# A one-layer hybrid kernel: its log-decay stage written in program order, weight copies a quarter later, a convolution's taps a step later, and one load moved ahead of two others

## The chip, the cores and the metric

The kernel runs on one core of one Trainium2 chip. The time is device microseconds of a whole execution, and the figure that counts is the median of several runs. Five engines work side by side, each through its own instructions in its own fixed order: PE multiplies matrices, DVE and POOL do element-wise arithmetic, ACT evaluates functions and copies, and SP issues the DMAs. An instruction that waits holds up everything behind it on its engine.

## What is computed

The reference is one transformer layer over 1024 tokens of width 1024. A gated linear attention (GLA) over chunks and a short convolution mix the tokens; a second part with a 3x3 convolution follows. The change touches the part around the attention's decay gates, which the reference states so:

```python
def gate_logdecay(a_low, w, b):
    a = (a_low @ w + b).astype(jnp.float32)
    return (jax.nn.log_sigmoid(a) / GLA_TAU).reshape(...)

def gla_final_state(k, v, g):                  # over the 256 context tokens
    b = jnp.cumsum(g.astype(jnp.float32), axis=1)
    w = jnp.exp(b[:, -1:] - b)
    return jnp.einsum('bthk,bthv->bhkv', k * w, v)

def token_mixers(p, s_f, s_b, ...):
    k, v, g_f, g_b = gla_inputs(p, ...)
    ...
    o_sc = sb * dwconv_row(sc * sx, w_sc, b_sc, rows, width)   # three taps along a row of 64
    return jnp.concatenate([o_gla, o_sc], axis=-1)             # then @ w_out
```

All matrix products that carry precision are made from two parts of each operand, a high part and a low part, with three multiplications (high by high, low by high, high by low).

## The kernel before

PE's order is written out by hand for the whole program. The other engines are ordered by a scheduler, which works from a simulated timing, except inside the `manual_schedule` blocks, where the named engines keep the order of the code.

**The stage around the change.** After the first projections two generators run side by side. `stream()` multiplies sixteen more 128-column blocks of the input projection (C_SC, C_SX and C_SB for each of four column groups j, then C_OG). `halves` runs a block: two halves of 512 tokens, each of them 24 matmuls that stop half way for a `yield`, so a block has four quarters of 12 matmuls. `gla()` computes the decays, the chunk states and the attention. After each of its steps it yields a number of quarters, and the loop at the end runs that many quarters of `stream()` in between. So PE alternates between a few small matmuls of `gla()` and 12 long ones of `stream()`.

**The log-decay steps.** Two context chunks (`ctx_decay`) and then eight chunks of tokens, c = 0 to 7 (`decay(c)`), pass through `logdecay`: PE makes 128x512 gate values in one of two banks `ps_at`; ACT applies Abs, Exp and Ln one after the other (tile `ge`); DVE makes `gc` or `g` from them, which frees the bank for the gate matmul after next. `ctx_keys(j)` lets PE sum `gc` by a triangle `tri` into a bank `ps_ms`, ACT take the exponential into `kw`, and DVE multiply. `sums(c)`, two steps behind `decay(c)`, sums `g` in a bank `ps_ms`, and ACT copies it to `bc`. There are two such banks, so each of these waits for ACT to empty the one before the last. `ctx_state` makes the start state. For the chunk states a tile `kx` is made of `bc` (DVE difference, ACT exponential, DVE product with the keys), once for each half of the tokens and each direction; PE turns it in `kx_turn` and multiplies it in `update`. `dec` holds the decays of whole chunks.

**Weights of `stream()`.** `stream_weights` loads a block (`wr`, 512 KB) while the block ahead is being multiplied, ACT copies the high part `wh`, and POOL makes the low part `wl` in four pieces, one after each quarter. There are two of each of these tiles. In the code the copy `wh` stands where the load stands, at the start of the block ahead.

**The short convolution.** `sc_first` keeps the C_SC half, `sc_conv` multiplies it by the C_SX half and applies three taps (ACT the middle one, DVE the two others), and `sc_last` multiplies by the C_SB half and stores it.

**What is ordered by hand before.** `ORDERED = 2`: DVE alone keeps the code's order for the first two steps of each generator. From there on ACT and DVE follow the scheduler.

**The output projection.** After the attention, a `manual_schedule` block of ACT, DVE and SP prepares the first two token tiles of the product with w_out: `so` (the stored convolution half of each of the two tiles, the second one in a part of `t7`), `sog` (the gate half, which passes through Silu in `mix_gate`), and the parts of w_out (`wo_split`). PE's first 24 matmuls use `so[0]`, the next 24 use `so[1]`, and only then come the products that need the gated half.

Of the kernel before, what the change touches and what calls it, by code (L numbers as in the profile page):

```python
# [21 lines left out]
P = 128  # L22
# [13 lines left out]
GW = 64  # L36
# [83 lines left out]
def build(nc, ap, out, dbg=None):  # L120
# [3 lines left out]
    def nm(s="t"):  # L124
        return f"{s}{next(names)}"

    def act(o, i, fn=AF.Copy, **kw):
        return S.activation(o, i, fn, **kw)  # L128
# [20 lines left out]
    with tile.TileContext(nc) as tc, tc.manual_schedule(engines={mybir.EngineType.PE}):  # L149
# [25 lines left out]
        def bank(n):  # L175
            return pools[n][1].tile([P, 512], F32, tag=n, name=nm("ps"))
# [7 lines left out]
        def col(name, j=0, n=1):  # L184
            o, w = COLS[name]
            return cols[:, o + j : o + j + n]
# [372 lines left out]
        def stream_weights(src, eng):  # L559
            raw = wp.tile([P, KT, P], F32, tag="wraw", name=nm("wr"))  # L560
            SY.dma_start(raw, src)
            hi = wp.tile([P, KT, P], F32R, tag="whi", name=nm("wh"))
            lo = wp.tile([P, KT, P], F32R, tag="wlo", name=nm("wl"))
            act(hi, raw)

            def rest():
                for k in range(0, KT, 2):
                    eng.tensor_tensor(lo[:, k : k + 2], raw[:, k : k + 2], hi[:, k : k + 2].bitcast(F32), ALU.subtract)  # L568
                    yield

            return hi, lo, rest()
# [67 lines left out]
        def halves(w, nxt, dests):  # L639

            hi, lo = w[:2]
            for hf in range(2):
                bk = bank(ps_mm)
                s = slice(hf * 512, hf * 512 + 512)
                for kt in range(KT):
                    mm3(bk, (hi[:, kt, :], lo[:, kt, :]), (hxh[kt][:, s], hxl[kt][:, s]), kt == 0, kt == KT - 1)
                    if kt == KT // 2 - 1:
                        next(nxt[2], None)
                        yield
                dests(hf, bk)  # L650
                next(nxt[2], None)
                yield

        def stream():
            w = w2
            for n in range(16):
# [8 lines left out]
                    yield from halves(w, nxt, lambda hf, bk: og_out(n - 12, hf, bk))  # L665
                w = nxt

        def sc_tile(dt=F32):
            return pg_.tile([P, 512], dt, tag="sc", bufs=4, name=nm("sc"))

# [4 lines left out]
        def sc_conv(j, hf, bk, us):  # L675
            u = us[hf]
            V.tensor_tensor(u, u, bk, ALU.mult)
            y = sc_tile()
            act(y, u, AF.Identity, bias=col("bsc", j), scale=col("wsc", 3 * j + 1))
            y3, u3 = (a.rearrange("p (r c) -> p r c", c=GW) for a in (y, u))  # L680
            V.scalar_tensor_tensor(y3[:, :, 1:], u3[:, :, :-1], col("wsc", 3 * j), y3[:, :, 1:], ALU.mult, ALU.add)
            V.scalar_tensor_tensor(y3[:, :, :-1], u3[:, :, 1:], col("wsc", 3 * j + 2), y3[:, :, :-1], ALU.mult, ALU.add)
            us[hf] = y

        def sc_last(j, hf, bk, us):
            y = us[hf]
# [28 lines left out]
            split(wo_raw(0), hi, lo)  # L715
            woh[worder[0]], wol[worder[0]] = hi, lo

        ORDERED = 2
        on = [None] * NT
        pe_ = popen("pe_", "right", bufs=1)  # L720
        flat = lambda t: t.rearrange("p f t -> p (f t)")
# [1 line left out]
        def gla():  # L723
# [26 lines left out]

            kxs, kxt = {}, {}

            def kx_prep(hf, d):
                e = (P - 1) if d == 0 else 0
                for hh in range(2):
                    act(decv[d * DK : d * DK + DK, hh, :, 4 * hf : 4 * hf + 4],
                        bc[hf][d][hh * DK : hh * DK + DK].rearrange("p f (c t) -> p f c t", t=P)[:, :, :, e],
                        AF.Exp, scale=ITAU)
                kx = pe_.tile([P, 2, 512], F32, tag="e", bufs=4, name=nm("kx"))
                b3 = bc[hf][d].rearrange("p f (c t) -> p (f c) t", t=P)  # L760
                V.tensor_tensor(kx.rearrange("p f (c t) -> p (f c) t", t=P),
                                b3[:, :, e : e + 1].broadcast_to([P, 8, P]), b3, ALU.subtract)
                act(kx, kx, AF.Exp, scale=ITAU)
                V.tensor_tensor(kx, kx, kh[hf], ALU.mult)
                kxs[hf, d] = kx

            def kx_turn(c):
                pt = bank(ps_at)
# [52 lines left out]
            for c in range(NT):  # L821
                decay(c)
                if c == 2:
                    V.tensor_copy(masks, mraw)
                if 0 < c <= NCT:
                    ctx_keys(c - 1)
                if c > 1:
                    sums(c - 2)
                if c == 4:
                    su = [px.tile([P, 2, 512], F32, tag="x", name=f"su{i}") for i in range(4)]  # L830
                    ctx_state()
                if c in (5, 6):
                    kx_prep(0, c - 5)
                yield 0.8 if c > 1 else 1
            sums(NT - 2)
            yield 0.8
# [1 line left out]
            for c in range(NT):  # L838
                kx_turn(c)
                if c == 1:  # L840
                    pclose("pgt")
                    pw = popen("pw", "left", bufs=1)
                    for n in range(3):
                        wo_raw(n)
                if c > 0:
                    update(c - 1)
                if c in (1, 2):
                    kx_prep(1, c - 1)
                yield 1.2
            update(NT - 1)  # L850

# [134 lines left out]
                    yield 0.8  # L986

        ga, st = gla(), stream()
        with tc.manual_schedule(engines={mybir.EngineType.DVE}):
            for _ in range(ORDERED):  # L990
                next(st)
                next(ga)
        due = 0.0
        for steps in ga:
            due += steps
            while due >= 1:
# [41 lines left out]
        def dma(dst, src):  # L1038
            behind[0] = SY.dma_start(dst, src).ins
# [7 lines left out]
        def gate_load(c):  # L1047
            sog = p2.tile([P, H, P], F32, tag="sog", bufs=2, name=nm("sog"))
            dma(sog, og_d[c // 4][c % 4])
            return sog  # L1050
# [6 lines left out]
        def mix_first(so):  # L1057
            mh = wp.tile([P, KT, P], F32R, tag="whi", name=nm("mh"))
            ml = wp.tile([P, KT, P], F32R, tag="wlo", name=nm("ml"))
            split(so, mh[:, 4:8, :], ml[:, 4:8, :])  # L1060
            return mh, ml
# [171 lines left out]
        with tc.manual_schedule(engines={mybir.EngineType.Activation, mybir.EngineType.DVE, mybir.EngineType.SP}):  # L1233
            so = pvo.tile([P, H, P], F32, tag="vo", name=nm("so")), t7[:, 0, :].rearrange("p (h t) -> p h t", t=P)
            dma(so[0], sc_d[0][0])
            sog = [gate_load(c) for c in range(2)]
            dma(so[1], sc_d[0][1])
            wo_raw(6)
            xts = [x1_load(c) for c in range(2)]
            wo_split(1)  # L1240
            made = [mix_first(so[0])]
            wo_split(2)
            wo_split(3)
            wo_raw(7)
            mix_gate(0, sog[0])
            made.append(mix_first(so[1]))
            wo_split(4)
            split(sog[0], *(t[:, 0:4, :] for t in made[0]))
            mix_gate(1, sog[1])
            wo_split(5)  # L1250
            wo_split(6)
            split(sog[1], *(t[:, 0:4, :] for t in made[1]))
            wo_split(7)
# [447 lines left out]
```

## Time and profile before

| what | us |
|---|---|
| median of 3 runs | 1142.1 |
| the three runs | 1141.63, 1142.1, 1143.94 |
| the profiled execution's own time | 1145.11 |
| its span, first to last instruction | 1143.3 |
| PE, DVE busy in the span | 1116.2, 874.5 |
| ACT, POOL busy in the span | 523.6, 490.1 |

The profiled execution took 1.8 us more than its span. Times inside the trace are counted from the start of the span. A matmul of 512 columns starts every 0.23 us where nothing holds PE up, though each is shown as 0.39 us long, since matmuls overlap. So the time that PE loses is read from the starts: the distance from one start to the next, less 0.23 us. In rows of the trace a number in brackets is the engine's idle time ahead of the row, and behind the arrow stands what ended it; where a row has "x2" or more, it merges neighbours of the same kind.

### The profile page before, as it was taken

Reading aid. Unit: us, or ns where it says so; the run is one execution under the profiler, and the core shown is the slowest. Engines: PE = TensorE matmul, PEld = TensorE weight load, DVE = VectorE, ACT = ScalarE, POOL = GpSimd, SP = SyncE. Lnnn points to the kernel's source line nnn. Section 1 sums busy time; section 2 is a strip of 40 time slices with the busy share of each in tenths; the row PEclk is TensorE's granted clock in tenths of the full one; section 3 lists DMA queues with packets and bytes.
Section 4 is the critical chain, followed back from the end, with each engine's and each line's share of the span. In section 5 each row is a group of like instructions: output and inputs, shape, how many; then the busy total and the mean of one; then the engine's idle time right before and its main releaser. Section 6 shows DMA issues by size and latency. Waiting matters only on the chain. (4 is left out here: it accounts for less than half of the span.)

```text
span 1143.3 us, 16858 instructions
## 1 busy us (share of the span) xinstructions
PE 1116.2 (98%) x6256; PEld 924.3 (81%) x6256; DVE 874.5 (76%) x1193; ACT 523.6 (46%) x941; POOL 490.1 (43%) x465
## 2 busy tenths in 40 slices
PE   8999989999999999999999999999999999999997
PEld 7689977888887878887888888888888888888885
DVE  5979845699777465677799887887878788777676
ACT  6744167654343366565323333324242445544443
POOL 5200031347466111128787787777778670000002
PEclk9999999999999999999999999999999999999999
DMA  9987962312113274231244223322323269978572
GB/s 354 303 284 243 348 108 58 95 43 67 53 32 102 62 245 145 83 125 66 86 148 142 98 83 111 124 98 74 120 99 106 79 228 353 333 241 287 189 240 101
DMA packets 80132, 176.00 MB, mean 154 GB/s; under 512 B 9807, under 2 KB 21711, under 8 KB 80050
## 3 DMA queue, kind: packets, MB, share of 16 engines
q1 hardware_dynamic: 80050, 174.93, 46.1%
q8 instruction: 49, 0.80, 0.3%
q14 instruction: 33, 0.27, 0.1%
HBM read 142.12 MB, written 32.78 MB: 153 GB/s over the span
## 5 line engine op out<-in xcount | busy, mean ns | idle before, releaser
L1373 DVE SCALAR_TENSOR_TENSOR y<-u,cols,y 128x945 f32<-128x945 f32 (+2 forms) x176 | 214.8, 1222 | 3.7 <-ACT y L128 1.3
L145 PE MATMUL ps<-mx,p 128*128 128x512 f32 x440 | 173.5, 394 | 0.9 <-DVE g L1428 0.5
L146 PE MATMUL ps<-mx,p 128*128 128x512 f32 x440 | 172.5, 392 | 0.0
L147 PE MATMUL ps<-mx,p 128*128 128x512 f32 x440 | 172.5, 392 | 0.0
L135 POOL TENSOR_TENSOR p<-rs,p 128x512 fp32r<-128x512 f32 x88 | 116.6, 1329 | 86.1 <-ACT p L128 86.1
L568 POOL TENSOR_TENSOR wl<-wr,wh 128x256 fp32r<-128x256 f32 x64 | 57.9, 935 | 163.6 <-ACT wh L128 163.5
L147 PE MATMUL ps<-p,p 128*128 128x512 f32 x308 | 120.0, 390 | 0.2
L146 PE MATMUL ps<-p,p 128*128 128x512 f32 x308 | 119.9, 389 | 0.0
L145 PE MATMUL ps<-p,p 128*128 128x512 f32 x308 | 119.9, 389 | 0.0
L145 PE MATMUL ps<-hxh,wh 128*128 128x512 f32 x256 | 104.0, 406 | 1.0 <-DVE sc L687 1.0
L147 PE MATMUL ps<-hxh,wl 128*128 128x512 f32 x256 | 100.8, 394 | 0.0
L145 PEld LDWEIGHTS ps<-mx,p 128*128 128x128 f32 x440 | 82.5, 188 | 22.5 <-ACT u L128 3.2
L146 PE MATMUL ps<-hxl,wh 128*128 128x512 f32 x256 | 100.6, 393 | 0.0
L128 ACT ACTIVATE p<-rs 128x512 fp32r<-128x512 f32 x88 | 54.5, 623 | 100.6 <-POOL rs L1198 100.6
L147 PEld LDWEIGHTS ps<-mx,p 128*128 128x128 f32 x440 | 82.6, 188 | 18.7
L146 PEld LDWEIGHTS ps<-mx,p 128*128 128x128 f32 x440 | 82.6, 188 | 18.2
L135 POOL TENSOR_TENSOR p<-wr,p 128x512 fp32r<-128x512 f32 x57 | 74.0, 1298 | 10.9 <-ACT p L128 10.9
L128 ACT ACTIVATE y<-u,cols 128x1024 f32<-128x1024 f32 x22 | 26.6, 1210 | 102.9 <-DVE u L1435 102.9
L147 PE MATMUL ps<-b,p 128*128 128x512 f32 x176 | 69.5, 395 | 0.0
L145 PE MATMUL ps<-b,p 128*128 128x512 f32 x176 | 69.4, 394 | 0.0
L146 PE MATMUL ps<-b,p 128*128 128x512 f32 x176 | 69.4, 394 | 0.0
L147 PEld LDWEIGHTS ps<-p,p 128*128 128x128 f32 x308 | 57.8, 188 | 12.9 <-DVE p L135 0.8
(278 smaller groups left out, 2611.8 us busy)
## 6 DMA issues: line engine op xcount, KB each, us to landing
ada<-in_ada SPq DMA_DIRECT2D x64, 512.0 KB, 5.3
wr<-in_wu SPq DMA_DIRECT2D x48, 512.0 KB, 4.0
h<-hd SPq DMA_DIRECT2D x77, 256.0 KB, 4.3
hd<-h SPq DMA_DIRECT2D x73, 256.0 KB, 2.0
wdr<-in_wd SPq DMA_DIRECT2D x55, 256.0 KB, 3.3
wdr<-in_wd SPq DMA_DIRECT2D x22, 512.0 KB, 6.0
x<-in_x SPq DMA_DIRECT2D x16, 512.0 KB, 4.5
wr<-in_wb SPq DMA_DIRECT2D x16, 512.0 KB, 3.7
```

The costliest lines, as they stand in the source:

```text
L128: return S.activation(o, i, fn, **kw)
L135: (eng or V).tensor_tensor(lo, raw, hi.bitcast(F32), ALU.subtract)
L145: PE.matmul(ps, lh, rh, start=first, stop=False, skip_group_check=more)
L146: PE.matmul(ps, lh, rl, start=False, stop=False, skip_group_check=more)
L147: PE.matmul(ps, ll, rh, start=False, stop=last, skip_group_check=more)
L568: eng.tensor_tensor(lo[:, k : k + 2], raw[:, k : k + 2], hi[:, k : k + 2].bitcast(F32), ALU.subtract)
L1373: V.scalar_tensor_tensor(y3[:, ro, co], u3[:, ri, ci], col("wcf", 9 * p + 3 * (dr_ + 1) + dc + 1), y3[:, ro, co], ALU.mult, ALU.add)
```

## The change

It has five parts. (1) ACT joins DVE in the hand-ordered block, and that block now covers eleven steps of `gla()` instead of two, with the quarters of `stream()` between them, so it reaches to the step of c = 7 and one step past it. (2) In `stream_weights` the copy `wh` moves from the start of the block ahead to the end of its first quarter. (3) `kx_prep` is cut into `kx_diff`, `kx_rest` and `chunk_decay`, which are put into different steps; the chunk decays come after all the sums. (4) The taps of the first convolution group (j = 0) are put off until the next half starts. (5) At the output projection, `so[1]` is loaded ahead of the two `sog` tiles, and it is split ahead of the first `mix_gate`.

```diff
@@ stream_weights
-            act(hi, raw)
 
             def rest():
+                act(hi, raw)
                 for k in range(0, KT, 2):
                     eng.tensor_tensor(lo[:, k : k + 2], raw[:, k : k + 2], hi[:, k : k + 2].bitcast(F32), ALU.subtract)
                     yield
@@ halves
             for hf in range(2):
+                for f in later:
+                    f()
+                later.clear()
                 bk = bank(ps_mm)
@@ sc_conv
             V.tensor_tensor(u, u, bk, ALU.mult)
-            y = sc_tile()
-            act(y, u, AF.Identity, bias=col("bsc", j), scale=col("wsc", 3 * j + 1))
...
+            def taps():
+                y = sc_tile()
+                act(y, u, AF.Identity, bias=col("bsc", j), scale=col("wsc", 3 * j + 1))
...
+            if j:
+                taps()
+            else:
+                later.append(taps)
@@ gla
-        ORDERED = 2
+        ORDERED = 9
...
-                if c in (5, 6):
-                    kx_prep(0, c - 5)
+                if c == 6:
+                    kx_diff(0, 1)
+                if c > 5:
+                    kx_rest(0, c - 6)
+                if c == 5:
+                    kx_diff(0, 0)
                 yield 0.8 if c > 1 else 1
...
                 if c in (1, 2):
-                    kx_prep(1, c - 1)
+                    kx_diff(1, c - 1)
+                    kx_rest(1, c - 1)
+                if c in (1, 2, 3, 4):
+                    chunk_decay((c - 1) // 2, (c - 1) % 2)
                 yield 1.2
...
-        with tc.manual_schedule(engines={mybir.EngineType.DVE}):
-            for _ in range(ORDERED):
+        due = 0.0
+        with tc.manual_schedule(engines={mybir.EngineType.Activation, mybir.EngineType.DVE}):
+            for _ in range(2):
                 next(st)
                 next(ga)
-        due = 0.0
+            for _ in range(ORDERED):
+                due += next(ga)
+                while due >= 1:
+                    next(st)
+                    due -= 1
@@ output projection
             dma(so[0], sc_d[0][0])
+            dma(so[1], sc_d[0][1])
             sog = [gate_load(c) for c in range(2)]
-            dma(so[1], sc_d[0][1])
...
+            made.append(mix_first(so[1]))
             mix_gate(0, sog[0])
-            made.append(mix_first(so[1]))
```

PE's order, matmul by matmul, is the same in both kernels, and so is POOL's. What moves is the order on ACT and DVE, and a few loads on SP.

**ACT, the two first chains.** These rows are ACT's, where the gates of the second context chunk (bank ps_1772, tile ge_1774) and of c = 0 (bank ps_1781, now ps_1780; tile ge_1783, now ge_1782) pass through Abs, Exp and Ln; "small" is the constant one of the Ln. Before:

```order
L128 ACTIVATE ge_1774<-ps_1772 128x512
L128 ACTIVATE ge_1783<-ps_1781 128x512
L128 ACTIVATE ge_1774<-ge_1774 128x512
L128 ACTIVATE ge_1783<-ge_1783 128x512
L128 ACTIVATE ge_1774<-ge_1774,small 128x512
L128 ACTIVATE ge_1783<-ge_1783,small 128x512
```

Now:

```order
L128 ACTIVATE ge_1774<-ps_1772 128x512
L128 ACTIVATE ge_1774<-ge_1774 128x512
L128 ACTIVATE ge_1774<-ge_1774,small 128x512
L128 ACTIVATE ge_1782<-ps_1780 128x512
L128 ACTIVATE ge_1782<-ge_1782 128x512
L128 ACTIVATE ge_1782<-ge_1782,small 128x512
```

The two chains were interleaved, and now the first one is finished ahead of the second.

**ACT, the copy of a weight block.** A little later on ACT: sc_1829 (now sc_1828) is the second kept C_SC half, ge_1835 (now ge_1834) the chain of c = 2, ge_1857 that of c = 3, kw the exponentials of the context keys (bank ps_1841, now ps_1840, is that of the second chunk), bc the copies of the sums, and wh_1872 (now wh_1871) the high part of the block of j = 0 and C_SB. Before:

```order
L128 ACTIVATE kw<-ps_1809 128x4x64 x2
L128 ACTIVATE wh_1872<-wr_1870 128x1024
L128 ACTIVATE sc_1829<-ps_1788 128x512
L128 ACTIVATE ge_1835<-ps_1833 128x512
L128 ACTIVATE kw<-ps_1841 128x4x64
L128 ACTIVATE ge_1835<-ge_1835 128x512
L128 ACTIVATE kw<-ps_1841 128x4x64
L128 ACTIVATE ge_1835<-ge_1835,small 128x512
L128 ACTIVATE bc_1741<-ps_1849 128x2x128
```

Now:

```order
L128 ACTIVATE ge_1834<-ps_1832 128x512
L128 ACTIVATE ge_1834<-ge_1834 128x512
L128 ACTIVATE ge_1834<-ge_1834,small 128x512
L128 ACTIVATE kw<-ps_1840 128x4x64 x2
L128 ACTIVATE bc_1741<-ps_1848 128x2x128
L128 ACTIVATE bc_1742<-ps_1848 128x2x128
L128 ACTIVATE ge_1857<-ps_1855 128x512
L128 ACTIVATE ge_1857<-ge_1857 128x512
L128 ACTIVATE ge_1857<-ge_1857,small 128x512
L128 ACTIVATE bc_1741<-ps_1862 128x2x128
L128 ACTIVATE bc_1742<-ps_1862 128x2x128
L128 ACTIVATE wh_1871<-wr_1869 128x1024
```

The copy of the weight block stood ahead of the second kw, and now stands two chains and two pairs of sums behind it; the second kw now stands behind the whole chain of c = 2.

**DVE, the last gate.** These rows are DVE's at the end of the eight chunks: g_1973 (now g_1968) are the gates of c = 6 and then of c = 7, kx_1990 (now kx_1983) the key tile of the first half of the tokens backwards, kx_1948 the one forwards, sc_1829 and sc_2007 (now sc_1828 and sc_2028) the second half of the first convolution group and its taps. Before:

```order
L482 SCALAR_TENSOR_TENSOR g_1973<-ps_1974,ge_1976 128x512
L761 TENSOR_TENSOR kx_1990<-bc_1742 128x1024
L677 TENSOR_TENSOR sc_1829<-sc_1829,ps_1959 128x512
L764 TENSOR_TENSOR kx_1990<-kx_1990,kh_90 128x1024
L681 SCALAR_TENSOR_TENSOR sc_2007<-sc_1829,cols,sc_2007 128x8x63
L682 SCALAR_TENSOR_TENSOR sc_2007<-sc_1829,cols,sc_2007 128x8x63
L482 SCALAR_TENSOR_TENSOR g_1973<-ps_2012,ge_2014 128x512
```

Now:

```order
L482 SCALAR_TENSOR_TENSOR g_1968<-ps_1969,ge_1971 128x512
L776 TENSOR_TENSOR kx_1983<-bc_1742 128x1024
L781 TENSOR_TENSOR kx_1948<-kx_1948,kh_90 128x1024
L682 TENSOR_TENSOR sc_1828<-sc_1828,ps_1954 128x512
L482 SCALAR_TENSOR_TENSOR g_1968<-ps_2001,ge_2003 128x512
L781 TENSOR_TENSOR kx_1983<-kx_1983,kh_90 128x1024
L688 SCALAR_TENSOR_TENSOR sc_2028<-sc_1828,cols,sc_2028 128x8x63
L689 SCALAR_TENSOR_TENSOR sc_2028<-sc_1828,cols,sc_2028 128x8x63
```

The gates of c = 7 stood behind the second product with the keys and two taps, and now stand ahead of these three.

More of the change, by code (lines that the diff above doesn't have):

```diff
@@ L666, in stream @@
                 w = nxt
+        later = []
         def sc_tile(dt=F32):
@@ L677, in sc_conv @@
             V.tensor_tensor(u, u, bk, ALU.mult)
-            y = sc_tile()
-            act(y, u, AF.Identity, bias=col("bsc", j), scale=col("wsc", 3 * j + 1))
[L680 to L683, printed above, removed]
+            def taps():
+                y = sc_tile()
+                act(y, u, AF.Identity, bias=col("bsc", j), scale=col("wsc", 3 * j + 1))
+                y3, u3 = (a.rearrange("p (r c) -> p r c", c=GW) for a in (y, u))
+                V.scalar_tensor_tensor(y3[:, :, 1:], u3[:, :, :-1], col("wsc", 3 * j), y3[:, :, 1:], ALU.mult, ALU.add)
+                V.scalar_tensor_tensor(y3[:, :, :-1], u3[:, :, 1:], col("wsc", 3 * j + 2), y3[:, :, :-1], ALU.mult, ALU.add)
+                us[hf] = y
+            if j:
+                taps()
+            else:
+                later.append(taps)
         def sc_last(j, hf, bk, us):
@@ L751, in gla, with chunk_decay @@
             kxs, kxt = {}, {}
-            def kx_prep(hf, d):
+            def chunk_decay(hf, d):
                 e = (P - 1) if d == 0 else 0
@@ L758, in kx_prep, with kx_diff, kx_rest @@
                         AF.Exp, scale=ITAU)
-                kx = pe_.tile([P, 2, 512], F32, tag="e", bufs=4, name=nm("kx"))
+            def kx_diff(hf, d):
+                e = (P - 1) if d == 0 else 0
+                kxs[hf, d] = pe_.tile([P, 2, 512], F32, tag="e", bufs=4, name=nm("kx"))
                 b3 = bc[hf][d].rearrange("p f (c t) -> p (f c) t", t=P)
-                V.tensor_tensor(kx.rearrange("p f (c t) -> p (f c) t", t=P),
+                V.tensor_tensor(kxs[hf, d].rearrange("p f (c t) -> p (f c) t", t=P),
                                 b3[:, :, e : e + 1].broadcast_to([P, 8, P]), b3, ALU.subtract)
-                act(kx, kx, AF.Exp, scale=ITAU)
-                V.tensor_tensor(kx, kx, kh[hf], ALU.mult)
-                kxs[hf, d] = kx
+            def kx_rest(hf, d):
+                act(kxs[hf, d], kxs[hf, d], AF.Exp, scale=ITAU)
+                V.tensor_tensor(kxs[hf, d], kxs[hf, d], kh[hf], ALU.mult)
             def kx_turn(c):
```

## The prediction

> **What bounds the kernel now.** I read the page first, then PE's groups, then PE's rows where it waits, and last what each wait goes back to on ACT and DVE.
>
> ```profile
> span 1143.3 us, 16858 instructions
> PE 1116.2 (98%) x6256; PEld 924.3 (81%) x6256; DVE 874.5 (76%) x1193; ACT 523.6 (46%) x941; POOL 490.1 (43%) x465
> ```
>
> PE is busy for 1116.2 of 1143.3 us and its order does not change, so an edit can pay only by closing a hole in PE's row: 27.1 us at most, and only the holes that this change reaches. PE's groups say where holes end:
>
> ```profile
> L743 PE MATMUL ps<-tri,g 128*128 128x128 f32 x64 | 8.5, 277 | 5.0 <-ACT kw L128 2.7 <-DVE g L482 2.3
> ...
> L145 PE MATMUL ps<-woh,mh 128*128 128x512 f32 x128 | 51.3, 401 | 0.3 <-ACT mh L128 0.3
> ```
>
> The first line is `sums`, the second the output projection: waits of 2.7, 2.3 and 0.3 us where the change acts. PE's own rows give their place and true size, and a fourth wait at a gate matmul:
>
> ```profile
> 158.82 0.39 PE L147 MATMUL ps<-hxh,wl 128*128 128x512 f32 x1
> 159.85 0.50 PE L473 MATMUL ps<-wgh,aT 98*128 98x512 f32 x1 [0.65 <-DVE gc L482]
> ...
> 164.22 0.40 PE L473 MATMUL ps<-wgh,aT 98*128 98x512 f32 x1
> ...
> 166.56 0.48 PE L473 MATMUL ps<-wgh,aT 98*128 98x512 f32 x1
> 169.74 1.16 PE L743 MATMUL ps<-tri,g 128*128 128x128 f32 x8 [2.70 <-ACT kw L128]
> 170.66 0.49 PE L145 MATMUL ps<-hxh,wh 128*128 128x512 f32 x1
> ...
> 175.08 0.39 PE L473 MATMUL ps<-wgh,aT 98*128 98x512 f32 x1
> ...
> 188.50 0.39 PE L473 MATMUL ps<-wgh,aT 98*128 98x512 f32 x1
> ...
> 193.04 0.39 PE L147 MATMUL ps<-hxh,wl 128*128 128x512 f32 x1
> 195.74 1.13 PE L743 MATMUL ps<-tri,g 128*128 128x128 f32 x8 [2.31 <-DVE g L482]
> ```
>
> Start to start, less the usual 0.23 us, the holes are 0.80, 2.95 and 2.47 us. The middle one has a tail:
>
> ```profile
> 170.97:174.35 3.38, 3.38 (x9) 2.62 (x8) 0.74 (x2) 2.04 (x5) 0.00 (x0) 0.50 0.59 160
> 177.91:180.76 2.85, 2.85 (x16) 2.34 (x14) 1.31 (x3) 0.61 (x2) 0.00 (x0) 1.00 0.00 0
> ```
>
> These are two stretches of PE (third number from the end: the granted clock). After the long hole the clock was 0.50 for 3.38 us; the second stretch is a whole quarter of 12 matmuls at full clock, 2.85 us. The quarter after the hole took longer: it began at 170.66, and the gate behind it came at 175.08, after 4.42 us. So the slow clock cost 1.57 us.
>
> **The change part by part.** *The first hole.* ACT's rows show a chain alone, and then the two that are interleaved:
>
> ```profile
> 153.17 0.60 ACT L128 ACTIVATE ge<-ps 128x512 f32<-128x512 f32 x1 [0.27 <-PE ps L473]
> ...
> 154.47 0.72 ACT L128 ACTIVATE ge<-ge,small 128x512 f32<-128x512 f32 x1
> ...
> 156.34 1.08 ACT L128 ACTIVATE ge<-ps 128x512 f32<-128x512 f32 x2
> 159.10 0.69 DVE L482 SCALAR_TENSOR_TENSOR gc<-ps,ge 128x512 f32<-128x512 f32 x1 [3.19 <-ACT ge L128]
> ```
>
> Alone it takes 2.02 us (153.17 to 155.19). Starting at 156.34 and no longer interleaved it ends at 158.36; DVE's 0.69 us follow 0.03 us later and end at 159.08; PE follows 0.06 us behind, as it did at 159.85, so at 159.14. PE's matmuls allow 159.05. **Gain 0.71 us.**
>
> *The second hole.* PE waits for the second kw on ACT, because a weight copy stands ahead of it there and waits for its load:
>
> ```profile
> 162.31 0.64 ACT L128 ACTIVATE kw<-ps 128x256 f32<-128x256 f32 x2
> 166.59 1.06 ACT L128 ACTIVATE wh<-wr 128x1024 fp32r<-128x1024 f32 x1 [3.64 <-DMA wr<-in_wb]
> ...
> 169.29 0.39 ACT L128 ACTIVATE kw<-ps 128x256 f32<-128x256 f32 x1
> ```
>
> Now only the kept half (0.6 us) and the chain of c = 2 stand ahead of kw. PE: gate c = 1 at 159.14, gate c = 2 4.37 us later as before (159.85 to 164.22) at 163.51, gate c = 3 at 165.85. ACT: the chains of c = 0 and c = 1 end at 160.28 and 162.20, the first kw at 162.8, the kept half (PE is done with it at 163.7) at 164.3. Independent ACT rows start 0.1 us before the last one ends, so the chain of c = 2 runs from 164.20 to 166.22, the second kw to 166.76, and PE goes on at 166.81 instead of 169.74. Of the 2.93 us, 0.71 are counted. **Gain 2.22 us**; a hole of 0.73 us is left, with ACT as its cause. A hole that short should leave the clock alone: the one of 2.47 us at 193.04 was followed by no slow matmuls, the one of 2.95 us was. **Gain 1.57 us.** [...]
>
> *The copy itself* goes behind the chain of c = 3. With PE 4.50 us early by now, ACT is through with the second pair of bc at 169.7, the copy runs to 170.7, and gate c = 4 (PE 170.6, its bank full at 171.0) finds ACT free. POOL's four pieces then end near 174; PE wants the block at 186. So the later copy costs nothing, covered by 12 us; each quarter uncovered would cost its 2.85 us.
>
> *The third hole.* DVE's rows ahead of the last gate, and ACT's exponential of a kx:
>
> ```profile
> 188.78 1.22 DVE L761 TENSOR_TENSOR kx<-bc 128x1024 f32<-128x1024 f32 x1
> ...
> 191.32 1.76 DVE L764 TENSOR_TENSOR kx<-kx,kh 128x1024 f32<-128x1024 f32 x1 [0.73 <-ACT kx L128]
> 193.01 1.21 DVE L681 SCALAR_TENSOR_TENSOR sc<-sc,cols,sc 128x504 f32<-128x504 f32 x1
> ...
> 194.91 0.68 DVE L482 SCALAR_TENSOR_TENSOR g<-ps,ge 128x512 f32<-128x512 f32 x1
> 190.23 1.06 ACT L128 ACTIVATE kx<-kx 128x1024 f32<-128x1024 f32 x1
> ```
>
> The product and the taps fill 191.32 to 194.91, and all three now stand behind the gate. PE makes the gates of c = 7 at 184.0 (188.50 less 4.50); ACT, which ends the first kx at 184.3, chains them to 186.4. DVE, which ends the gates of c = 6 at 183.4, has a difference (1.22), a product as long, which waits for the exponential until 184.3, and the convolution's product (0.7, as the gates' row) ahead of it, and is through at 186.4; so g is ready at 187.2. PE comes to `sums` at 188.77 (193.27 less 4.50). **Gain 2.47 us**, with 1.6 us in hand. What is late next is the second kx: ACT's exponential, behind a pair of bc (0.65, as kw's), ends at 187.95, DVE's product at 189.2, and `kx_turn` wants it at 189.7.
>
> *The output projection.*
>
> ```profile
> 401.72 0.39 PE L147 MATMUL ps<-woh,ml 128*128 128x512 f32 x1
> 402.44 0.50 PE L145 MATMUL ps<-woh,mh 128*128 128x512 f32 x1 [0.33 <-ACT mh L128]
> ...
> 403.50 0.39 PE L145 MATMUL ps<-woh,mh 128*128 128x512 f32 x1
> 396.90 1.47 SPq L1039 DMA_DIRECT2D sog<-ogd  x2
> 398.46 0.38 SPq L1039 DMA_DIRECT2D t<-scd  x1
> 397.38 1.28 ACT L128 ACT_TABLE_LOAD   x1
> ...
> 401.75 0.63 ACT L128 ACTIVATE mh<-t 128x512 fp32r<-128x512 f32 x1 [0.83 <-DMA t<-scd]
> ```
>
> Four matmuls from 401.72 to 403.50 take 1.78 us instead of 0.91. The load t was issued at 398.46 and used at 401.75; issued in the place of sog, at 396.90, it is there by 400.19, ACT's 0.63 and DVE's low part (0.7, as the gates' row) end by 401.5, and PE wants it at 401.95. **Gain 0.87 us.** Silu with its table load (1.28) moves behind that copy and so ends about 2 us later; its product is wanted by PE after another 24 matmuls, 5.5 us on, so about 3 us of cover are left, and each microsecond beyond them would cost one.
>
> *At nothing:* the taps put off (their result is wanted a block later), the chunk decays (first used by the recurrences, after `kx_turn`), the masks' cast (DVE idles around it), the w_out loads ahead of a block load on SP (for a block that is multiplied two blocks later). If a tap were uncovered it would cost its 0.74 us.
>
> **The sum:** 0.71 + 2.22 + 1.57 + 2.47 + 0.87 = 7.84 us. The profiled execution of 1145.11 us would take 1137.3. It is 3.0 us above the median of 1142.1, and nothing shows where; I take those 3.0 us to lie elsewhere, so that the median becomes 1142.1 - 7.8 = **1134.3 us**.
>
> **The rivals.**
>
> *The clock did not fall in the timed runs of before.* Then 6.27 us go: 1135.8. For it: one trace shows one such stretch, and the three times differ by 2.3 us. Chance 0.18.
>
> *The profiled execution's 3.0 us lie in these very holes*, since the load that held ACT up took long. Then 4.8 us go: 1137.3. For it:
>
> ```profile
> row<-gv SPq DMA_DIRECT2D x2, 4.0 KB, 13.7
> DMA to landing us min/median/max: 12.5/13.4/14.4
> wr<-in_wb SPq DMA_DIRECT2D x16, 512.0 KB, 3.7
> ```
>
> These are the two loads ahead of the block's on SP, of the block loads issued from 150 to 171 us the time to landing, and the page's row of all block loads: 14.4 us at worst here, where the block loads of the whole run have a median of 3.7. A load of 4.0 KB that takes 13.7 us may vary. Chance 0.14.
>
> *The stage behind takes the gain back.* PE arrives 7 us early at a stage where DVE is nearly full:
>
> ```profile
> 240.00:260.00 20.00, 20.00 (x205) 15.98 (x204) 19.67 (x34) 7.28 (x9) 10.85 (x13) 1.00 0.14 41
> 340.00:360.00 20.00, 18.55 (x198) 14.67 (x196) 19.93 (x23) 8.77 (x10) 18.20 (x18) 1.00 0.30 81
> ```
>
> DVE (the third pair) is busy 19.67 and 19.93 of 20 us, and in the second stretch PE idles 1.45 us. If DVE set the pace, only the 0.87 us stay: 1141.2. Against it: PE idles nothing in the first stretch, and DVE too comes to it 7 us early, since it waited for the same sums. Chance 0.08.
>
> *The change doesn't do what it says*, if the holes had other causes: 1142.1. Against it are the rows of ACT and DVE in the new order. Chance 0.03.
>
> *Slower: the copy of the block at the head of ACT's queue.* In program order nothing may pass it; behind it stand the chain of c = 4 and the bc that frees a bank for the next `sums`, which PE wants at 176.5. Counting back through that bc, the chain and the copy, a load that lands after 172.5 costs microsecond for microsecond, and after 180.3 more than all is lost: landing at 184 it would be 1145.8. The slowest landing seen was 14.4 us, at 166.2, so it needs 28.5. Chance 0.03.
>
> **How the numbers follow.** The forecast has the rest, 0.54. A measurement of this kernel can tell about 0.2% from no change, 2.3 us: below 1139.8 is faster. The forecast and the first two rivals lie there, 0.86; the third and fourth are the same, 0.11; slower 0.03. The range goes up to 1139.5, past the second rival by a hole of 2 us that may stay at `kx_turn` or kw, and down to 1132.0, where a second slow stretch (1.57 us), after the hole at 193, would have been in the timed runs, and 0.7 us for my replay.
>
> **What would show it.** In the profile of after: the gate of c = 1 near 159.1 with no wait; `sums` after the gate of c = 3 with a wait below 1 us, put down to ACT; clock 1.00 from 160 to 180; no wait of `sums` for DVE g; a quarter of `stream()` at 189 that stood at 196; the same distance of 7 us at 380; no wait for mh in the output projection. I am wrong if ACT, now in program order, waits for a `wr` or `kx` while PE waits for ACT, or if the 7 us shrink between 200 and 390.

## The result, and the profile after

The changed kernel takes **1137.37 us** (median of 4 runs, 1135.42 to 1137.5) beside 1141.87 us of the kernel before (4 runs, 1141.5 to 1143.94): a ratio of 0.995, with a 95% interval from 0.993 to 0.997. Two later sets of runs gave 1136.22 us (6 runs, beside 1143.36, ratio 0.9944, interval 0.9928 to 0.996) and 1135.71 us (5 runs, beside 1141.99, ratio 0.9943, interval 0.9931 to 0.9955). So the change is worth 4.5 to 7.1 us. The forecast was 1134.3 with a range from 1132.0 to 1139.5.

The profiled execution of the changed kernel took 1137.5 us. Its span, the busy time of each engine, and two of PE's groups:

```profile
span 1135.7 us, 16859 instructions
PE 1113.8 (98%) x6256; PEld 922.7 (81%) x6256; DVE 873.6 (77%) x1193; ACT 524.3 (46%) x941; POOL 491.6 (43%) x465
```

```profile
L145 PE MATMUL ps<-woh,mh 128*128 128x512 f32 x128 | 51.1, 400 | 0.0
...
L755 PE MATMUL ps<-tri,g 128*128 128x128 f32 x64 | 8.4, 276 | 0.5 <-ACT kw L128 0.5
```

`sums` (now L755) waited 5.0 us and waits 0.5; the output projection waited 0.3 and waits not at all. PE's own rows at the four places, and then two windows of PE (the third number from the end is the granted clock):

```profile
158.22 0.50 PE L473 MATMUL ps<-wgh,aT 98*128 98x512 f32 x1
...
164.93 0.48 PE L473 MATMUL ps<-wgh,aT 98*128 98x512 f32 x1
165.89 1.16 PE L755 MATMUL ps<-tri,g 128*128 128x128 f32 x8 [0.48 <-ACT kw L128]
...
187.81 1.05 PE L755 MATMUL ps<-tri,g 128*128 128x128 f32 x8
```

```profile
160.00:180.00 20.00, 19.52 (x114) 1.00 0.30 69
180.00:200.00 20.00, 20.00 (x119) 1.00 0.43 127
```

The gate of c = 1 and the eighth `sums` no longer wait, and the second `sums` has a hole of 0.73 us left (0.96 from start to start), put down to ACT. In the kernel before the same two windows read 0.91 and 1.00 for the clock:

```profile
160.00:180.00 20.00, 17.30 (x89) 0.91 0.41 72
180.00:200.00 20.00, 17.69 (x101) 1.00 0.19 54
```

Since PE's order is the same, the two traces can be laid side by side, matmul by matmul; a step in the distance between them is time gained there. The changed execution was 0.92 us ahead before the stage began (chance in the prelude). A hole's gain is read at the first matmul behind it. The first numeric column is the forecast, the second this pair of profiles; the third is another pair, *before_again* and *after_third* below:

| place | forecast | first pair | another pair |
|---|---|---|---|
| first hole (gate c = 1) | 0.71 | 0.71 | 0.71 |
| second hole (second `sums`) | 2.22 | 2.22 | 0.18 |
| slow clock | 1.57 | 1.61, behind the second hole | 1.73, behind the third |
| third hole (eighth `sums`) | 2.47 | 2.46 | 2.46 |
| output projection | 0.87 | 0.90 | 0.83 |
| sum | 7.84 | 7.90 | 5.91 |

Between the stage and the output projection the distance doesn't shrink: 8.00 us at 196 and 8.06 at 390, both with the 0.92 of the prelude. Of the first pair 1.4 us are given back between 500 and 525, where short waits in the second part differ between executions; in the other pair 0.4 are given back there. The first set's median for the changed kernel is 1.2 to 1.7 us above the two later ones. Its profiled execution lost 1.5 us in a slow stretch of the clock in the prelude (118.8 to 122.2), which *after_third* doesn't have.

### The profile page after: what moved, and what is told of

Its sections match the earlier page's. It is cut to its first block, busy times and chain, and to the rows that moved or that the text cites. A ratio compares the mean times of both kernels' runs of the same rounds, so it can differ in the third digit from the quotient of the medians.

```text
span 1135.7 us, 16859 instructions
## 1 busy us (share of the span) xinstructions
PE 1113.8 (98%) x6256; PEld 922.7 (81%) x6256; DVE 873.6 (77%) x1193; ACT 524.3 (46%) x941; POOL 491.6 (43%) x465
## 5 line engine op out<-in xcount | busy, mean ns | idle before, releaser
L146 PE MATMUL ps<-mx,p 128*128 128x512 f32 x440 | 172.5, 392 | 0.0
L147 PE MATMUL ps<-mx,p 128*128 128x512 f32 x440 | 172.5, 392 | 0.0
```

The costliest lines, as they stand in the source:

```text
L146: PE.matmul(ps, lh, rl, start=False, stop=False, skip_group_check=more)
L147: PE.matmul(ps, ll, rh, start=False, stop=last, skip_group_check=more)
```

## The experiments

Medians of one set share one chip and the runs of the kernel before.

| kernel | median us (runs) | before | ratio (95% interval) |
|---|---|---|---|
| before_again | 1143.8 (12) | 1143.36 | 1.001 (0.9995 to 1.0025) |
| after_again | 1136.22 (6) | 1143.36 | 0.9944 (0.9928 to 0.996) |
| rows_late | 1144.43 (12) | 1143.36 | 1.0009 (0.9993 to 1.0024) |
| no_load_ahead | 1137.59 (8) | 1143.36 | 0.9961 (0.9945 to 0.9978) |
| no_hand_order | 1136.22 (6) | 1142.57 | 0.9944 (0.9928 to 0.9961) |
| taps_early | 1140.08 (8) | 1142.57 | 0.9971 (0.9958 to 0.9985) |
| before_rows_twice | 1148.76 (4) | 1142.57 | 1.0052 (1.0033 to 1.0072) |
| after_rows_twice | 1135.78 (4) | 1142.57 | 0.9939 (0.9919 to 0.9959) |
| after_third | 1135.71 (5) | 1141.99 | 0.9943 (0.9931 to 0.9955) |
| no_hand_again | 1136.27 (5) | 1141.99 | 0.9947 (0.9935 to 0.9959) |
| kw_first | 1135.66 (5) | 1141.99 | 0.9949 (0.9936 to 0.9961) |
| taps_late_only | 1139.57 (12) | 1141.99 | 0.9973 (0.9959 to 0.9986) |

**The two kernels once more.** *before_again* and *after_again* are unchanged copies.

> The kernel of before once more, for a second profile and its times. The forecast took the holes of the first profile (0.80, 2.95 and 2.47 us, and 3.38 us at clock 0.50) to be those of every execution. If so, this profile has a hole of 2.7 to 3.1 us ahead of the second sums and of 2.3 to 2.6 us ahead of the eighth, and a span near 1140 (the median less 1.8) comes from elsewhere. If the first profile was an unlucky one in these holes (second rival), the second sums wait at least 1 us less and the weight load lands well ahead of 166.2. If only the clock differs (first rival), the hole is the same and the clock stays at 1.00 behind it, which takes 1.6 us off.

> The changed kernel once more. By the forecast's terms the wait of the second sums is 0.7 us with ACT as its cause, no wait of the eighth, no wait in the output projection. Time against before 0.995 to 0.997 with more runs. The two waits at the start of the second part (0.70 and 0.92 us from start to start beyond the usual 0.23, at 503.4 and 518.2) that the first profile of after has and before has not (there 0 and 0.63): if they come of chance in the landing of a load, this profile has them smaller or not at all; if the change makes them, they are there again within 0.2 us.

PE's rows of *before_again* at the second and the third hole, and three windows of it, the second of them behind the third hole:

```profile
164.53 0.48 PE L473 MATMUL ps<-wgh,aT 98*128 98x512 f32 x1
165.64 1.16 PE L743 MATMUL ps<-tri,g 128*128 128x128 f32 x8 [0.63 <-ACT kw L128]
...
190.03 1.83 PE L743 MATMUL ps<-tri,g 128*128 128x128 f32 x8 [2.31 <-DVE g L482]
```

```profile
187.00:190.00 3.00, 0.73 (x4) 1.00 0.30 68
190.20:193.80 3.60, 3.60 (x16) 0.53 0.46 135
...
196.40:199.20 2.80, 2.80 (x18) 1.00 0.70 240
```

The second hole was 0.88 us here (1.11 from start to start), not 2.95, and no slow clock followed it. The third was as long as before, and now the slow clock came behind it: 0.53 over 3.6 us, of which 3.41 were at 0.50. So the size of the second hole and the place of the slow clock belong to one execution and not to the kernel. *after_again* repeats the changed kernel's profile: one hole of 0.73 us in the stage. Of the two waits in the second part the one at 503 is gone and the other one is 0.68 us instead of 0.92, so they vary from execution to execution.

**Why the weight load was late.** *rows_late* is the kernel before with two small stores of a gate row, which SP issues just ahead of the load, put behind the load of a later block.

```diff
-            SY.dma_start(raw, src)
+            wdma.append(SY.dma_start(raw, src).ins)
...
-            SY.dma_start(d.rearrange("f p -> p f"), row_scale(gt0, gname))
+            with tc.issue_after(wdma[4]):
+                SY.dma_start(d.rearrange("f p -> p f"), row_scale(gt0, gname))
```

> Before, with the two small scattered stores (4 KB each, issued at 150.5 and 151.1) put behind the load of the block after next on SP, and nothing else moved. Theory A, they hold up the weight load whose copy ACT waits for: the load issued at about 151.3 then lands within 6 us instead of 14.4, ACT copies it at 164.4 when PE has let the tile go, the second kw ends near 167.5, and the hole ahead of the second sums falls from 2.95 to about 0.8 us with no slow clock behind it: 2.2 us, or 3.8 with the clock, off the profile. The eighth sums still wait 2.4 us. Theory B, the load is late for another reason (bandwidth): it still lands after 164, and the hole stays.

The load's row (KB, us to landing) in the kernel before, in *before_again* and in *rows_late*:

```profile
wr<-in_wb SPq DMA_DIRECT2D x1, 512.0 KB, 14.4
```

```profile
wr<-in_wb SPq DMA_DIRECT2D x1, 512.0 KB, 11.3
```

```profile
wr<-in_wb SPq DMA_DIRECT2D x1, 512.0 KB, 4.3
```

Behind the stores the load takes 11.3 or 14.4 us, without them 4.3. In the nine other profiles with the two stores ahead of it, it took 11.2 to 12.6: the profiled execution of the kernel before had the latest load of all. Yet *rows_late* is no faster than the kernel before, since its second hole is the same 0.88 us as in *before_again*:

```profile
164.63 1.06 ACT L128 ACTIVATE wh<-wr 128x1024 fp32r<-128x1024 f32 x1 [1.59 <-issue]
```

ACT makes the copy at 164.63, though the load landed at 155.14 (issued at 150.85, 4.3 us later). It no longer waits for the load. The same wait stands ahead of the copy in *before_again* (1.60 us), and there it is put down to a matmul of PE. So with a load that is in time the hole comes from a copy that waits for PE and stands ahead of the second kw, and an earlier load gains nothing more.

**The stores doubled.** Each of the two stores issued twice, the other one to a tile that nobody reads; in the kernel before (*before_rows_twice*) and in the changed one (*after_rows_twice*).

```diff
-            d = dr.tile([KT, P], F32, name=nm("row"))
-            SY.dma_start(d.rearrange("f p -> p f"), row_scale(gt0, gname))
+            d, d2 = (dr.tile([KT, P], F32, name=nm("row")) for _ in range(2))
+            v = row_scale(gt0, gname)
+            SY.dma_start(d2.rearrange("f p -> p f"), v)
+            SY.dma_start(d.rearrange("f p -> p f"), v)
```

> The kernel before with each of the two small scattered stores of a gate row issued twice (the second copy to a tile that nobody reads), ahead of the weight load on SP. It asks whether the second hole is set by these stores. Theory A (they delay the load, and the copy at ACT's head of line passes the delay to PE): the load lands some 10 us later (near 174 instead of 163.5), and the second sums wait for kw 10 to 12 us instead of 2.7; time 8 to 12 us over the kernel before. Theory B (the load is slow for another reason, or the stores overlap): landing within 2 us of before, second hole 1 to 4 us, time within 2 us.

> The changed kernel with the same doubled stores. It puts the rival that ended slower to the test: the copy at the head of ACT's queue, which in my account costs microsecond for microsecond from a landing after 172.5. Theory A (copy covered until then): the load lands near 174 and the stage loses 1 to 2 us at sums for ACT bc, so the time is 0 to 3 us over the changed kernel and 8 or more under the kernel before with the same stores. Theory B (no such cover; ACT's queue stops PE as soon as the copy waits, from 169.3): 4 to 6 us lost. Theory C (the load doesn't move): nothing lost.

ACT's copy and PE's `sums` in the kernel before with doubled stores, then the same in the changed kernel:

```profile
167.97 1.06 ACT L128 ACTIVATE wh<-wr 128x1024 fp32r<-128x1024 f32 x1 [7.68 <-DMA wr<-in_wb]
...
171.11 1.23 PE L743 MATMUL ps<-tri,g 128*128 128x128 f32 x4 [6.71 <-ACT kw L128]
```

```profile
165.64 1.16 PE L755 MATMUL ps<-tri,g 128*128 128x128 f32 x8 [0.47 <-ACT kw L128]
...
169.60 1.05 PE L755 MATMUL ps<-tri,g 128*128 128x128 f32 x8
...
169.80 1.06 ACT L128 ACTIVATE wh<-wr 128x1024 fp32r<-128x1024 f32 x1 [1.22 <-DMA wr<-in_wb]
```

The load came 4 to 6 us earlier than I expected of four stores, but the mechanism is plain: before, ACT stood 7.68 us at the copy and PE 6.71 us at `sums`; after, ACT stood 1.22 us at the copy and PE lost nothing by it (I had expected 1 to 2 us). Doubled, the stores cost the kernel before 6.2 us (expected: 8 to 12); the changed kernel stays 6.8 us under the kernel before, as without them (6.3 in the set of *after_third*), and the two differ by 13.0 us. This put the rival that ended slower to a test with the copy's start at 169.80: its cover holds there. The point from which it costs, a landing after 172.5, was not reached.

**Without the hand order.** *no_hand_order* and *no_hand_again* are one kernel: the changed one with the loop of part 1 as it was; parts 2 to 5 stay.

```diff
-        due = 0.0
-        with tc.manual_schedule(engines={mybir.EngineType.Activation, mybir.EngineType.DVE}):
+        with tc.manual_schedule(engines={mybir.EngineType.DVE}):
             for _ in range(2):
                 next(st)
                 next(ga)
-            for _ in range(ORDERED):
...
+        due = 0.0
```

> The changed kernel, with only the hand order (part 1) taken out; parts 2 to 5 stay. ACT's rows then stand as in the kernel before at the first two holes (the two chains interleaved, the weight copy ahead of the second kw), while on DVE the gates of c = 7 stay ahead of the product and the taps. Theory A (holes one and two belong to the hand order of ACT alone, hole three to where the taps and the product stand on DVE): against the changed kernel the first hole of 0.7 us and the second one (0.9 to 2.9 us, by when the weight load lands) are back, the wait of the eighth sums for DVE g is still gone, the output projection does not wait for mh; the time lies 2.5 to 3.5 us under the kernel before, 3 to 5 above the changed one. Theory B (the later weight copy of part 2 closes the second hole by itself): the second hole stays at 0.7 us or less, the time within 1 us of the changed kernel. Theory C (the hand order closes the third hole): the wait for DVE g of 2.3 us is back.

> The changed kernel once more, as the yardstick for the three kernels that run beside it: 1136 to 1137.5 us, one hole of 0.73 us at the second sums in the stage, no wait for DVE g.

> The changed kernel without the hand order once more, beside the changed kernel on the same chip. Theory A (the hand order is worth its two holes, 0.77 us at the gate of c = 1 and 0.15 or more at the second sums): 0.9 us over the changed kernel in its fast loads, up to 2.5 in executions whose weight load is late; median 1 to 1.5 us over. Theory B (the hand order is worth nothing, other waits take its place): medians within 0.5 us.

*no_hand_again* on PE, and on ACT around the weight copy:

```profile
157.58 0.50 PE L473 MATMUL ps<-wgh,aT 98*128 98x512 f32 x1 [0.61 <-DVE gc L482]
...
165.41 1.16 PE L755 MATMUL ps<-tri,g 128*128 128x128 f32 x8 [0.64 <-ACT kw L128]
...
187.34 1.05 PE L755 MATMUL ps<-tri,g 128*128 128x128 f32 x8
```

```profile
162.26 1.06 ACT L128 ACTIVATE wh<-wr 128x1024 fp32r<-128x1024 f32 x1 [1.59 <-PE ps L147]
163.22 0.58 ACT L128 ACTIVATE sc<-ps 128x512 f32<-128x512 f32 x1
163.70 0.59 ACT L128 ACTIVATE ge<-ps 128x512 f32<-128x512 f32 x1
164.18 0.39 ACT L128 ACTIVATE kw<-ps 128x256 f32<-128x256 f32 x1
```

The first two holes are back, the third is not, and the copy stands ahead of the second kw although part 2 is in: part 2 without the hand order doesn't move it. (Neither part 2 alone in the kernel before nor the hand order without part 2 was run.) But the size I expected was wrong. Laid beside *after_third*, the two holes are worth 0.71 and 0.18 us, the medians differ by 0.56 us in one set and by nothing between sets, and neither can be told from no change. I had expected 3 to 5, and then 1 to 1.5: all loads were in time here (11.2 and 12.1 us). What the hand order buys beyond 0.9 us is, as the doubled stores suggest, that a late load does no harm; the kernel without the hand order was not run with a late load.

**The third hole.** *taps_early* undoes part 4 in the changed kernel (`if j:` becomes `if True:`), *taps_late_only* adds part 4 alone to the kernel before (the lines of `sc_conv`, `later` and `halves` in the diff above).

> The changed kernel with part 4 undone: the taps of the first convolution group stand at once behind their product, on ACT ahead of the chain of c = 7 and on DVE ahead of its g. In the changed kernel g of c = 7 is made 1.6 us before its sums want it. Theory A (the taps matter for the third hole): ACT's tap waits for the product (186.0 in the changed kernel), the chain starts 0.8 us later than the tap, DVE g ends near 189.5 and the eighth sums wait about 1.2 us for it. Theory B (the hand order and the cut kx of parts 1 and 3 suffice, the 1.6 us cover the taps): no wait, same time as the changed kernel. In both, the holes one and two stay closed as in the changed kernel.

> The kernel before with part 4 alone: the taps of the first convolution group put off until the next half. On DVE the gates of c = 7 then stand ahead of the two taps, but still behind the product with the keys. Theory A (the third hole is made of what stands ahead of g on DVE): of its 2.47 us the taps' 1.9 us go, 0.5 to 0.9 stay; the first two holes stay as in the kernel before; 2 to 3.5 us under the kernel before, the more where the slow clock no longer follows. Theory B (the product and ACT's exponential ahead of it set g): the third hole stays at 2 us or more, time within 1 us of the kernel before.

The eighth `sums` and the first `kx_turn` in *taps_early*, the eighth `sums` in *taps_late_only*:

```profile
188.52 1.13 PE L755 MATMUL ps<-tri,g 128*128 128x128 f32 x8 [1.56 <-DVE g L482]
189.49 0.38 PE L788 MATMUL ps<-ident,kx 128*128 128x128 f32 x2
190.45 0.47 PE L788 MATMUL ps<-ident,kx 128*128 128x128 f32 x2 [0.59 <-DVE kx L781]
```

```profile
187.91 1.13 PE L755 MATMUL ps<-tri,g 128*128 128x128 f32 x8 [0.39 <-DVE g L482]
```

With the taps ahead of g the wait returns (a hole of 1.72 us; the 1.6 us by which g was early are spent and 1.7 more), a second one follows at kx, the slow clock comes behind them, and the median is 2.5 us under the kernel before, where the changed kernel is 6.3 under it in the set of *after_third*. With part 4 alone the third hole shrinks from 2.47 to 0.55 us, by the 1.9 us that the taps take in DVE's rows, no slow clock follows, and the kernel is 2.4 us under the kernel before.

**The load ahead.** *no_load_ahead* is the changed kernel with `so[1]` loaded and split where it was.

```diff
-            dma(so[1], sc_d[0][1])
             sog = [gate_load(c) for c in range(2)]
+            dma(so[1], sc_d[0][1])
...
-            made.append(mix_first(so[1]))
             mix_gate(0, sog[0])
+            made.append(mix_first(so[1]))
```

> The changed kernel without its fifth part: so[1] is loaded and split behind the gates again. If that part is worth its term, the output projection's matmuls lose 0.87 us again where the second token tile starts (a wait put down to mh), and all else in the log-decay stage is as in after. If its gain was given back at the start of the second part, the waits at 503 and 518 are gone here and the time is the same as after or less; otherwise it is about 0.9 us (0.08%) more, which the times alone can hardly tell.

```profile
393.40 0.39 PE L147 MATMUL ps<-woh,ml 128*128 128x512 f32 x1
394.80 0.50 PE L145 MATMUL ps<-woh,mh 128*128 128x512 f32 x1 [1.01 <-ACT mh L128]
```

The wait for mh is back, and longer than in the profile of before, where it was 0.33. With the old order of loads it lies between 0.25 us (*before_again*) and 1.04 (*rows_late*): this term hangs on a load too. PE loses 1.56 us there beside *after_third*, where the two pairs above show 0.90 and 0.83. The median is 1137.59 beside 1136.22 of *after_again*, 1.4 us, which the intervals don't tell apart.

**The hole that is left.** *kw_first* puts the second kw pair on ACT ahead of the Ln of c = 2.

```diff
             act(e, e, AF.Exp, scale=-1.0)
+            between()
             act(e, e, AF.Ln, bias=one)
...
-                logdecay(gates_psum(c * P), gts[c])
+                logdecay(gates_psum(c * P), gts[c], (lambda: ctx_keys(1)) if c == 2 else lambda: None)
...
-                if 0 < c <= NCT:
-                    ctx_keys(c - 1)
+                if c == 1:
+                    ctx_keys(0)
```

> The changed kernel, with the second kw pair on ACT ahead of the last function (Ln) of the chain of c = 2, so that the bank of the second sums is emptied 0.7 us earlier; nothing else moves. Theory A (the hole left in the stage is ACT's order): the hole of 0.73 us at the second sums shrinks to 0.1 or less and the later rows of PE stand 0.6 us earlier to the end of the stage; the time is 0.6 us less, under what the runs can tell apart. Theory B (the delayed Ln takes it back): g of c = 2 is 0.7 us later, and a wait of about 0.6 us appears at the gate matmul of c = 4 or at the sums of c = 2.

```profile
164.29 0.48 PE L473 MATMUL ps<-wgh,aT 98*128 98x512 f32 x1
164.61 1.05 PE L756 MATMUL ps<-tri,g 128*128 128x128 f32 x8
```

The hole is gone (0.32 from start to start instead of 0.96) and nothing takes it back in the stage: beside *after_third*, PE gains 0.74 us there, at the hole and within these `sums`, and keeps it to 500. The medians, 1135.66 and 1135.71, can't tell 0.6 us.

## Why the prediction was right, and where it was not

**What bounds, and where.** Right: the gain came from four holes in PE's row and one slow stretch. By the signs that were named: the gate of c = 1 stands at 158.22, which with the 0.92 us of the prelude is the 159.14 of the working; the hole at the second `sums` is the 0.73 us of the working, on ACT; the clock is 1.00 from 160 to 180; the eighth `sums` stands at 187.81, with the prelude 188.73 against 188.77. The stage behind took nothing back.

**First hole, third hole, output projection** (0.71, 2.47, 0.87): right in place and size in both pairs, and each came back when its cause did: the first without the hand order, the third with the taps ahead of g, the last without the load ahead. For the third, I gave the credit to product and taps together, which the runs divide: added alone, part 4 is worth 1.92 us (2.47 less 0.55). The rest belongs to part 3, since the hole is closed in *no_hand_order* too, which has both parts and not the hand order.

**Second hole** (2.22): the mechanism is right, as the doubled stores show from both sides, but as a term of the median it was mis-sized. It was measured in an execution whose load took 14.4 us. Of the five profiles with ACT's old order and stores of the old number and place, the other four (*before_again*, *taps_late_only* and the two without the hand order) had holes of 0.87 to 0.89 us; the change leaves 0.73, so it is worth about 0.15 there.

**The step that failed** is the last of the sum: "nothing shows where; I take those 3.0 us to lie elsewhere". In the second hole the profile of before lost 2.04 us (2.22 less 0.18) that the other profiles without a late load did not lose, which is two thirds of the 3.0, if those profiles stand for the median. Laid beside *before_again*, an execution 3.66 us shorter, it also lost 1.5 us in a slow stretch of the prelude (119.8 to 123.2). The second rival had put all 3.0 us into the holes and gave 1137.3, and I held it for 0.14. With the 5.9 us of the other pair the median of 1142.1 would become 1136.2, close to the later medians of 1136.22 and 1135.71.

**The slow clock** (1.57): right in size, for a wrong reason. I took a hole of 2.47 us to be too short for it, since it "was followed by no slow matmuls"; but behind the same hole the clock fell in *before_again* and *rows_late*. What differed is where the hole fell (last section). In all four profiles with this third hole the stage has one slow stretch, behind the second hole or the third: it moves and stays. The rival that the timed runs lack this term can be held against their mean clocks on record, where one stretch of 3.41 us at 0.50 is worth 0.0015. In the set of *after_third* all 17 runs of the kernel before lie at 0.997 or below, and all 5 of the changed kernel at 0.998 or above; in the set of *before_again*, 7 of 25 runs of the kernel before lie at 0.998 or above. A stretch in the prelude lowers this mean too, so it says only that most runs probably had the stretch and that some had not.

**The copy at nothing**, and the rival with it at the head of ACT's queue: right as far as tried, to a copy that starts at 169.80. **That the change does what it says** holds, but for part 2: without part 1 the copy stays where it was. Whether part 1 would move it without part 2 was not run.

## What to carry to other kernels

Before a wait in one profile becomes a term for the median, ask whether what it waits for has a time that varies, and look at more than one execution: the terms that came from a fixed order on an engine were right to 0.1 us; of the two that hung on a load, the second hole was right in one profile of five, and the output projection's was 0.83 to 1.56 us against 0.87. A copy that waits for a load should stand on an in-order engine behind all that PE needs soon: here it cost about 0.15 us with a load in time, 2.22 with one that took 14.4 us and more than 6 with the stores doubled. And where several parts are changed at once, add and remove them one at a time: here the smallest one, two taps put off, brings 2.4 us of the median gain.

## What the runs showed of the hardware

**Two small scattered stores held up a large load behind them.** Two stores of 4 KB, written as single numbers of 4 bytes (from 150.2 to 153.0 us the kernel before has 2082 transfers of this size, and *rows_late*, where the stores stand behind, has 16 under 512 B), made a load of 512 KB take 11.2 to 14.4 us instead of 4.3; four of them held it longer still, so that its copy waited until 167.97 in the kernel before and 169.80 in the changed one. The stores themselves took 13.5 to 14.0 us to land in the kernel before, and 11.9 to 12.4 in the changed one, though they move 4 KB each.

**The clock fell behind holes of 1.72 to 6.96 us, and not behind all of them.** Each slow stretch behind a hole of this stage lasted 3.41 us (6.83 in *before_rows_twice*) at a clock of 0.50; in the two pairs above it cost 1.61 and 1.73 us:

| profile | second hole | third hole | slow stretch |
|---|---|---|---|
| before | 2.95 | 2.47 | 171.0 to 174.4 |
| before_again | 0.88 | 2.46 | 190.3 to 193.7 |
| rows_late | 0.88 | 2.47 | 192.6 to 196.0 |
| before_rows_twice | 6.96 | 2.46 | 169.3 to 176.1 |
| taps_early | 0.73 | 1.72 | 190.7 to 194.1 |
| taps_late_only | 0.87 | 0.55 | none |

The changed kernel, with no hole over 0.73 us in the stage, has none: its clock is 1.00 from 160 to 200. In *taps_early* the slow stretch came behind a hole of 1.72 us with one of 0.8 behind it.

In the kernel before and with its stores doubled only the first of the two long holes was followed, and the traces show what differed. In the kernel before, every change of the granted clock lies a whole multiple of 3.413 us behind the first one (31, 32, 46, 47 and 330 of them), and in the changed kernel too (31, 32 and 328). Cut into pieces of this length, so that the slow stretch is one of them, the kernel before and then *before_again* read as follows (length, PE's busy time, clock):

```profile
167.57:170.98 3.41, 1.24 (x10) 1.00 0.05 19
191.46:194.87 3.41, 1.97 (x9) 1.00 0.17 12
194.87:198.29 3.42, 2.55 (x17) 1.00 0.51 168
```

```profile
186.86:190.27 3.41, 1.10 (x6) 1.00 0.35 92
190.27:193.68 3.41, 3.41 (x15) 0.50 0.43 123
```

In the kernel before, PE idles 2.17 us in the piece to 170.98, and the next one, to 174.40, has a clock of 0.50. The third hole lies across such a point, so PE idles 1.44 us in one piece and 0.87 in the next, and no slow clock follows. In *before_again* the same hole lies within one piece, which idles 2.31 us, and the next piece is slow. In *rows_late* it lies within the piece to 192.6, where the slow stretch begins. In *before_rows_twice*, counted on from its slow stretch, the third hole is divided too, into 1.08 and 1.23. So in these four profiles the hole of about 2.5 us was followed by a slow stretch where it fell into one piece (in the pair above that cost 1.73 us), and by none where it was divided. How much idle time it takes was not shown: in the prelude a piece that idles 1.50 us in the kernel before, and one that idles 1.53 in the changed kernel, are each followed by a slow one as well.
